# A two-layer trunk on one core: the second stage of a triangular inversion as a pipeline over four groups, and the values' convolution as a step of its own

## The chip, the cores and the metric

The kernel runs on one core of a Trainium2 chip. Its engines are PE (TensorE, matrix products), DVE (VectorE), ACT (ScalarE), POOL (GpSimd) and SP (SyncE, which starts DMA transfers). The metric is the device time of one execution in microseconds (us).

## The reference

Two layers act on 256 tokens of width 2048 in float32: h = h + Mixer(RMSNorm(h)). Layer 0 is a gated DeltaNet with 16 heads of 128, layer 1 is chunked softmax attention. What matters here is layer 0, cut to its core:

```python
proj = h @ w_in                                  # q, k, v, gate z, decay a, beta b
qkv  = silu(causal_depthwise_conv(qkv, conv_w))  # 4 taps
q, k = l2_norm(q) * 128 ** -0.5, l2_norm(k)
lower = where(tri_strict, (k * beta) @ k.T * decay, 0)
sol  = triangular_solve(eye + lower, rhs)        # rhs: v * beta and k * beta * exp(gc)
...
o = rms_norm(o, out_norm_w) * silu(z)
h = h + o @ w_out
```

The kernel solves over blocks of 128 tokens instead of 64: with two blocks for each of 16 heads it needs the inverses of 32 unit lower-triangular matrices of 128 x 128.

## The kernel before, in words

All weight products read 512 KB chunks of weights. `fetch` loads one (L208), ACT casts it to its high part (`whi`, L209) and DVE subtracts to get the low part (`wlo`, L210). Four load buffers and three of each part rotate, so a cast into a `whi` buffer waits until PE has used the chunk that was there three chunks earlier. The products themselves are all recorded at L259. In the stage of interest each chunk is of kind "half": 8 matmuls of 512 columns with `whi`, and 8 of 256 columns with `wlo`.

Everything else ("small work") is written as generators. `tick` and `step` take one piece of them after every part of a chunk, in turn from two lists, `bgq` and `bg2`; `drain()` takes pieces until both lists are empty. A list scheduler then sets each engine's final order; within an engine instructions run in that order.

`inversion()` has two stages. The first (L654 to L670) inverts the four 32 x 32 blocks on the diagonal of all 32 matrices on DVE. The second joins them:

- `lower` products (L684): 32 x 32 products of the matrix's off-diagonal blocks with the inverted blocks, two per matrix, on the array's tiles (0, 32) and (64, 96). DVE scales them into `v1` (L689).
- copies of the inverted blocks into the result `tt` and its transposed part `t64` (L696, L698), by ACT and POOL.
- corner products (L706, L708): three 32 x 32 products per matrix, from `v1`, on three tiles; ACT copies them to `tt` and `t64` (L713, L715). L706 writes one PSUM tile, L708 another.
- first quarter product (L723): a 64 x 64 product per matrix on tile (0, 64), from `t64`; DVE scales it into `v2` (L725).
- second quarter product (L731): 64 x 64 on tile (64, 0), from `v2` and `tt`; ACT copies the result to `tt` (L733).

Lower and corner products go in two groups of 16 matrices, each quarter pass in four groups of 8, one pass after the other. PE records every one of these float32 products as two matmuls, so 64 products stand as x128 in the profile.

After the inversion come the values. For each group of four heads, `pair` computes 512 columns of the projection, `v_small` convolves them (`conv`, L527 and L529), applies SiLU (L779), transposes (L786), scales by the key norms (L788), multiplies by the inverses `tt` (L795) and corrects the second block (L802, L805). `v_back` forms the output (L818 to L820), squares and normalises it (L821 to L830, L844 or L836), and `gated` transposes (L856) and splits it (L860, L861) for the output projection. For the last group the gate is multiplied in `za_small` (L752). After the first `pair` of values the main program calls `drain()`. The output projection's first products need heads 0 to 11 and are followed by those that need heads 12 to 15.

Of the kernel before, what the change touches and what calls it, by code (L numbers as in the profile page):

```python
# [10 lines left out]
AF = mybir.ActivationFunctionType  # L11
ALU = mybir.AluOpType
# [27 lines left out]
def tile_hybrid_trunk(  # L40
# [12 lines left out]
    act, dve, pool, pe = nc.scalar, nc.vector, nc.gpsimd, nc.tensor  # L53
# [9 lines left out]
    def ps_small():  # L63
        return pss.tile([P, 512], F32, name="pss", tag="pss")
# [19 lines left out]
    ps = ps_small()  # L84
# [169 lines left out]
    def drain():  # L254
        while now or bgq or bg2:
            step()
# [380 lines left out]
    def inversion():  # L637
        m = imem["m"]
        m1 = m[:, :4096].rearrange("p (k a b) -> p k a b", k=4, a=32)
        m2 = m[:, 4096:]  # L640
        tt = slot("tt", 16).rearrange("p (a c) -> p a c", c=P)
        tmem["tt"] = tt
        stg, lb, xb, tmp = (m1[:, i] for i in range(4))
        xr = m2[:, 0:1024].rearrange("p (a b) -> p a b", b=32)
        xt = m2[:, 1024:2048].rearrange("p (a b) -> p a b", b=32)
        t64 = m2[:, 2048:4096].rearrange("p (a b) -> p a b", b=64)
        yield from gather(12, H)
        xbf = xb.rearrange("p a b -> p (a b)")
# [24 lines left out]

        def diag(hh, r0, c0, n):
            c0 += T * (hh % 2)
            return dl[r0:r0 + n, hh // 2, 0, c0:c0 + n]


        for q0 in range(0, 32, 16):
            ps = ps_small()  # L680
            for i in range(16):
                for b in (0, 2):
                    r, c = 32 * b, 32 * b + 32
                    pe.matmul(ps[c:c + 32, i * 32:(i + 1) * 32], lhsT=diag(q0 + i, r, c, 32),  # L684
                              rhs=xr[r:r + 32, q0 + i, :], start=True, stop=True, tile_position=(r, c))
                if i == 7:
                    yield 1
            for c in (32, 96):
                dve.tensor_tensor(out=v1[c:c + 32, q0:q0 + 16, :],  # L689
                                  in0=ps[c:c + 32].rearrange("p (a b) -> p a b", b=32),  # L690
                                  in1=nbr_f[c:c + 32, q0:q0 + 16].unsqueeze(2).broadcast_to([32, 16, 32]),
                                  op=ALU.mult)
            yield 1
            for b in (2 * (q0 // 16), 2 * (q0 // 16) + 1):
                pr = slice(32 * b, 32 * b + 32)
                (pool.tensor_copy if b % 2 else act.copy)(out=tt[pr, :, 32 * b:32 * b + 32], in_=xt[pr])  # L696
                if b < 2:
                    act.copy(out=t64[pr, :, 32 * b:32 * b + 32], in_=xr[pr])  # L698
                yield 1
        for q0 in range(0, 32, 16):  # L700
            ps, ps2 = ps_small(), ps_small()
            for i in range(16):
                hh = q0 + i
                for b in (0, 2):
                    r, c = 32 * b, 32 * b + 32
                    pe.matmul(ps[r:r + 32, i * 32:(i + 1) * 32], lhsT=v1[c:c + 32, hh, :],  # L706
                              rhs=xt[c:c + 32, hh, :], start=True, stop=True, tile_position=(c, r))
                pe.matmul(ps2[32:64, i * 32:(i + 1) * 32], lhsT=xt[32:64, hh, :], rhs=v1[32:64, hh, :],  # L708
                          start=True, stop=True, tile_position=(32, 32))
                if i % 4 == 3 and i < 15:  # L710
                    yield 1
            for r in (0, 64):
                act.copy(out=tt[r:r + 32, q0:q0 + 16, r + 32:r + 64],  # L713
                         in_=ps[r:r + 32].rearrange("p (a b) -> p a b", b=32))
            act.copy(out=t64[32:64, q0:q0 + 16, 0:32], in_=ps2[32:64].rearrange("p (a b) -> p a b", b=32))  # L715
            yield 1
            yield 1

        v2 = m1[64:128].rearrange("p k a b -> p (k a b)")[:, 0:2048].rearrange("p (a b) -> p a b", b=64)
        for q0 in range(0, 32, 8):  # L720
            ps = ps_small()
            for i in range(8):
                pe.matmul(ps[64:128, i * 64:(i + 1) * 64], lhsT=diag(q0 + i, 0, 64, 64), rhs=t64[0:64, q0 + i, :],  # L723
                          start=True, stop=True, tile_position=(0, 64))
            dve.tensor_tensor(out=v2[:, q0:q0 + 8, :], in0=ps[64:128].rearrange("p (a b) -> p a b", b=64),  # L725
                              in1=nbr_f[64:128, q0:q0 + 8].unsqueeze(2).broadcast_to([64, 8, 64]), op=ALU.mult)
            yield 1
        for q0 in range(0, 32, 8):
            ps = ps_small()
            for i in range(8):  # L730
                pe.matmul(ps[0:64, i * 64:(i + 1) * 64], lhsT=v2[:, q0 + i, :], rhs=tt[64:128, q0 + i, 64:128],  # L731
                          start=True, stop=True, tile_position=(64, 0))
            act.copy(out=tt[0:64, q0:q0 + 8, 64:128], in_=ps[0:64].rearrange("p (a b) -> p a b", b=64))  # L733
            yield 1
        pool.tensor_scalar(out=epq, in0=ssq, scalar1=EPS, scalar2=EPS * P, op0=ALU.add, op1=ALU.mult)


# [30 lines left out]
                step()  # L768
        return pre

    def v_small(gi, ps):
        for cv in conv(ps, 32 + 4 * gi):
            yield 1
        if gi == 0:
            gated_tiles()
        vb, vs, on, sq = (dl_work(k) for k in range(4))
        tt, l01, z = tmem["tt"], dl[:, :, 0, P:2 * P], zmem["z"]
        h0 = 4 * gi
        act.activation(out=cv, in_=cv, func=AF.Silu)  # L779
        yield 1  # L780
        yield 1
        for p in range(2):
            ps = ps_small()
            for i in range(2):
                for t in range(2):
                    pe.transpose(ps[:, i * T + t * P:i * T + (t + 1) * P],  # L786
                                 cv[:, 2 * p + i, t * P:(t + 1) * P], ident)
            dve.tensor_tensor(out=vb[:, 2 * p:2 * p + 2], in0=ps.rearrange("p (h t d) -> p h t d", h=2, t=2),  # L788
                              in1=rk[:, h0 + 2 * p:h0 + 2 * p + 2, :].unsqueeze(3).broadcast_to([P, 2, 2, P]),
                              op=ALU.mult)  # L790
        yield 1
        for t in range(2):
            ps = ps_small()
            for i in range(4):
# [16 lines left out]
    def v_back(gi):  # L811
# [3 lines left out]
        for p in range(2):  # L815
            for i in (2 * p, 2 * p + 1):
                a, o = dec[:, h0 + i, :], po[p][:, (i % 2) * T:(i % 2 + 1) * T]
                pe.matmul(o[:, 0:P], lhsT=a[:, 0:P], rhs=vs[:, i, 0, :], start=True, stop=True)  # L818
                pe.matmul(o[:, P:T], lhsT=a[:, P:T], rhs=vs[:, i, 0, :], start=True, stop=False)
                pe.matmul(o[:, P:T], lhsT=a[:, T:T + P], rhs=vs[:, i, 1, :], start=False, stop=True)  # L820
            act.activation(out=sq[:, 2 * p:2 * p + 2], in_=po[p].rearrange("p (h t d) -> p h t d", h=2, t=2),  # L821
                           func=AF.Square)
        yield 1

        so = tiny.tile([P, 4, 2], F32, name="so", tag="so")
# [58 lines left out]
        bg2.append(za_small(gi, block("tokens", xb, 2)))  # L884
    for gi in range(4):
        ps = pair(xb, 2)
        if gi == 0:
            drain()
        bgq.append(v_small(gi, ps))
    bgq.append(za_small(3, block("tokens", xb, 2)))  # L890


# [318 lines left out]
```

## Time and profile before

| | |
|---|---|
| median of 3 timed runs | 1014.46 us (1013.89 to 1014.59) |
| profiled execution, first to last instruction (its span) | 1012.6 us |
| PE, matmuls | 1003.2 us, x6090 |
| PE, weight loads | 881.2 us, x6090 |
| DVE | 688.4 us, x1117 |
| ACT | 525.8 us, x778 |
| mean granted PE clock | 0.997 |

The profile gives the profiled execution's span but no other time for it; the three timed runs are executions of their own. PE's matmuls overlap: a matmul's row shows the time from its start to its modelled end, so the distance from start to start tells what it costs. The inversion's second stage lies between about 298 and 332 us of the span, the values' steps between 332 and 470.

### The profile page before, as it was taken

To read this page: it belongs to the slowest core of one execution; us is meant where nothing else is said; L and a number is where in the kernel's file an instruction comes from. 1 tells how busy PE (TensorE), PEld (TensorE's weight loads), DVE (VectorE), ACT (ScalarE), POOL (GpSimd) and SP (SyncE) were. 2 spreads that over 40 slices of the span, in tenths; PEclk is the share of its full clock that TensorE was granted. 3 is DMA by queue.
4 is the path that set the end of the run, shared out by engine and by line. 5 is a ranking of instruction groups with operands and counts; after the bars stand their busy time and mean duration, and the time that the engine had idled before them with its cause. 6 is when DMAs were issued, how large, how long until landed. Compare 5 with 4: busy or idle time off the path is not lost.

```text
span 1012.6 us, 15650 instructions
## 1 busy us (share of the span) xinstructions
PE 1003.2 (99%) x6090; PEld 881.2 (87%) x6090; DVE 688.4 (68%) x1117; ACT 525.8 (52%) x778; POOL 64.7 (6%) x83
## 2 busy tenths in 40 slices
PE   8999999999998999999999999999999999999998
PEld 7988888888887989899988888888888888889987
DVE  7789879997997587755866555444456665666554
ACT  7467865564454455444654444444445555555432
POOL 1000001131000011001000000000011010101000
PEclk9999999999998999999999999999999999999999
DMA  9665665555754454546756776666665555555472
GB/s 307 166 170 157 173 180 154 152 160 155 205 165 122 125 162 132 164 146 194 234 179 184 225 214 207 193 200 189 193 187 177 150 170 163 166 152 161 156 232 91
DMA packets 134186, 177.57 MB, mean 175 GB/s; under 512 B 7904, under 2 KB 90208, under 8 KB 134112
## 3 DMA queue, kind: packets, MB, share of 16 engines
q1 hardware_dynamic: 132672, 172.12, 57.4%
q0 software_dynamic: 1152, 4.19, 1.2%
q8 instruction: 47, 0.77, 0.3%
q10 hardware_dynamic: 288, 0.26, 0.1%
q14 instruction: 27, 0.22, 0.1%
HBM read 174.46 MB, written 2.10 MB: 174 GB/s over the span
## 4 chain that ended last, share of the span: by engine, by line
PE 97%; DVE 1%; issue 1%; DMA 1%; SPq 0%; ACT 0%; DVEq 0%
PE psp L259 85%; PE pss L601 2%; PE pss L259 1%; PE pss L795 1%; PE pss L1030 1%; PE pss L1049 1%; PE pss L1085 1%; DMA wt<-in_a_w_in_dram 1%; PE pss L501 1%; PE pss L1075 1%; PE pss L723 0%; PE pss L731 0%; DVE wlo L210 0%; PE pss L786 0%; PE pss L818 0%
## 5 line engine op out<-in xcount | busy, mean ns | idle before, releaser
L210 DVE TENSOR_TENSOR wlo<-wt,whi 128x1024 fp32r<-128x1024 f32 (+1 forms) x322 | 390.9, 1217 | 243.3 <-ACT whi L209 240.5
L209 ACT CAST whi<-wt 128x1024 fp32r<-128x1024 f32 (+1 forms) x322 | 336.5, 1046 | 386.3 <-PE psp L259 326.9
L259 PE MATMUL psp<-whi,xb 128*128 128x512 f32 x1024 | 318.7, 391 | 0.0
L259 PE MATMUL psp<-xb,whi 128*128 128x512 f32 (+1 forms) x1088 | 260.9, 382 | 1.3 <-ACT whi L209 0.7
L259 PEld LDWEIGHTS psp<-xb,whi 128*128 128x128 f32 x1088 | 196.1, 190 | 35.8 <-ACT whi L209 1.2
L259 PEld LDWEIGHTS psp<-whi,xb 128*128 128x128 f32 x1024 | 191.8, 188 | 39.1
L259 PE MATMUL psp<-wlo,xb 128*128 128x512 f32 x512 | 200.9, 392 | 0.0
L259 PE MATMUL psp<-xb,wlo 128*128 128x256 f32 x1024 | 148.9, 285 | 0.8 <-DVE wlo L210 0.8
L259 PE MATMUL psp<-g,whi 128*128 128x256 f32 (+1 forms) x736 | 149.5, 318 | 0.0
L259 PEld LDWEIGHTS psp<-xb,wlo 128*128 128x128 f32 x1024 | 138.4, 193 | 6.3 <-DVE wlo L210 1.0
L259 PEld LDWEIGHTS psp<-g,whi 128*128 128x128 f32 x736 | 121.5, 191 | 8.2
L259 PEld LDWEIGHTS psp<-wlo,xb 128*128 128x128 f32 x512 | 96.1, 188 | 19.7
L259 PE MATMUL psp<-g,wlo 128*128 128x256 f32 x480 | 101.9, 284 | 0.0
L259 PEld LDWEIGHTS psp<-g,wlo 128*128 128x128 f32 x480 | 77.8, 191 | 1.1
L529 DVE SCALAR_TENSOR_TENSOR cv<-raw,sm,cv 128x255 f32<-128x255 f32 (+2 forms) x144 | 62.8, 475 | 5.8 <-ACT cv L527 5.7
L527 ACT ACTIVATE cv<-raw,sm 128x256 f32<-128x256 f32 x48 | 22.1, 508 | 20.0 <-DVE raw L345 19.9
L1013 POOL TENSOR_SCALAR ssn<-ssn,uh 128x4 f32<-128x4 f32 x16 | 8.3, 529 | 266.8 <-DVE ssn L1011 266.8
L330 DVE TENSOR_TENSOR ev<-psp,ev 128x512 f32<-128x512 f32 x33 | 22.5, 681 | 0.0
L329 ACT COPY ev<-psp 128x512 f32<-128x512 f32 x33 | 19.1, 578 | 0.0
L830 POOL TENSOR_TENSOR ro<-so,nhalf 128x8 f32<-128x8 f32 x4 | 9.0, 2248 | 151.9 <-DVE so L828 151.9
L1061 ACT ACTIVATE raw<-raw,mx 128x128 f32<-128x128 f32 (+1 forms) x32 | 14.2, 445 | 7.4 <-DVE mx L1059 7.4
L605 DVE TENSOR_TENSOR dl<-pss,dl 128x512 f32<-128x512 f32 (+1 forms) x32 | 16.3, 549 | 2.7 <-PE pss L601 2.7
(233 smaller groups left out, 743.3 us busy)
## 6 DMA issues: line engine op xcount, KB each, us to landing
wt<-in_b_w_in_dram SPq DMA_DIRECT2D x128, 512.0 KB, 3.8
wt<-in_a_w_in_dram SPq DMA_DIRECT2D x127, 512.0 KB, 4.0
wt<-in_a_w_out_dram SPq DMA_DIRECT2D x32, 512.0 KB, 3.8
wt<-in_b_w_out_dram SPq DMA_DIRECT2D x32, 512.0 KB, 3.8
dl<-in_xT_dram POOLq DMA_DIRECT2D x4, 512.0 KB, 6.1
dl<-in_relb_dram POOLq DMA_DIRECT2D x4, 512.0 KB, 5.2
g<-in_xT_dram SPq DMA_DIRECT2D x7, 256.0 KB, 5.5
out_dram<-cv SPq DMA_DIRECT2D x2, 512.0 KB, 3.2
```

What stands on the lines that cost most here:

```text
L209: cast = act.copy(out=hi[:, js, cs], in_=wt[:, js, cs])
L210: rest = dve.tensor_tensor(out=lo[:, js, cs], in0=wt[:, js, cs], in1=hi[:, js, cs].bitcast(F32), op=ALU.subtract)
L259: state["mm"] = pe.matmul(*args, **kw).ins
L329: act.copy(out=ev, in_=ps[:, :, 1, :])
L330: dve.tensor_tensor(out=ev, in0=ps[:, :, 0, :], in1=ev, op=ALU.add)
L501: pe.matmul(dst, lhsT=lhs, rhs=rbuf[:, gi % 2, 2 * half + part, :], start=(part == 0), stop=(part == 1))
L527: act.activation(out=cv[:, i, :], in_=raw[:, i, :], func=AF.Copy, scale=conv_w(i0 + i, 3))
L529: dve.scalar_tensor_tensor(out=cv[:, i, s:], in0=raw[:, i, :T - s], scalar=conv_w(i0 + i, 3 - s), in1=cv[:, i, s:], op0=ALU.mult, op1=ALU.add)
L601: pe.matmul(dst, lhsT=kq[:, a, i, c:c + P], rhs=rhs, start=(n == 0), stop=(n == 2))
L605: dve.tensor_tensor(out=dl[:, h, :, c], in0=src.rearrange("p (k c) -> p k c", k=2), in1=dec[:, h, c].unsqueeze(1).broadcast_to([P, 2, n]), ...
L795: pe.matmul(ps[:, i * P:(i + 1) * P], lhsT=tt[:, 2 * (h0 + i) + t, :], rhs=vb[:, i, t, :], start=True, stop=True)
L1061: act.activation(out=s[:, a:b], in_=s[:, a:b], func=AF.Exp, bias=mx[:, t:t + 1], accum_out=sums[:, t:t + 1])
```

## The change

The second stage becomes four groups of 8 matrices. In round n it runs the quarter products for group n - 2 (first pass) and group n - 3 (second pass), then the corners of group n - 1, then the lower products of group n. The two quarter passes of a round alternate matrix by matrix and write the two halves of one PSUM tile. The third corner product now shares a PSUM tile with the other two. The copies of the diagonal blocks come in the first round. The convolution and SiLU of the values are a generator of their own, `v_conv`, in list `bg2`; `v_rest` holds the other steps and waits for it. `vmem` keeps the two within two groups of one another. The call of `drain()` after the first `pair` is gone.

```diff
-        for q0 in range(0, 32, 16):
-            ps = ps_small()
-            for i in range(16):
-                for b in (0, 2):
-                    ...
...
+        def lower(g):
+            q0 = 8 * g
+            ps = ps_small()
+            for i in range(8):
+                for b in (0, 2):
+                    r, c = 32 * b, 32 * b + 32
+                    pe.matmul(ps[c:c + 32, i * 32:(i + 1) * 32], lhsT=diag(q0 + i, r, c, 32),
+                              rhs=xr[r:r + 32, q0 + i, :], start=True, stop=True, tile_position=(r, c))
...
+        def corners(g):
...
-                pe.matmul(ps2[32:64, i * 32:(i + 1) * 32], lhsT=xt[32:64, hh, :], rhs=v1[32:64, hh, :],
+                pe.matmul(ps[32:64, i * 32:(i + 1) * 32], lhsT=xt[32:64, hh, :], rhs=v1[32:64, hh, :],
...
+        def quarters(g3, g4):
+            ps = ps_small()
+            for i in range(8):
+                cs = slice(i * 64, (i + 1) * 64)
+                if g3 is not None:
+                    hh = 8 * g3 + i
+                    pe.matmul(ps[64:128, cs], lhsT=diag(hh, 0, 64, 64), rhs=t64[0:64, hh, :],
+                              start=True, stop=True, tile_position=(0, 64))
+                if g4 is not None:
+                    hh = 8 * g4 + i
+                    pe.matmul(ps[0:64, cs], lhsT=v2[:, hh, :], rhs=tt[64:128, hh, 64:128],
+                              start=True, stop=True, tile_position=(64, 0))
+                if i == 3:
+                    yield 1
...
+        for n in range(7):
+            if n >= 2:
+                yield from quarters(n - 2 if n < 6 else None, n - 3 if n > 2 else None)
+            if 1 <= n <= 4:
+                yield from corners(n - 1)
+            if n < 4:
+                yield from lower(n)
+            if n == 0:
+                yield from copies()
...
-    def v_small(gi, ps):
+    vmem = {"turned": -1, "back": -1}
+    def v_conv(gi, ps):
+        while vmem["turned"] < gi - 2:
+            yield 1
         for cv in conv(ps, 32 + 4 * gi):
             yield 1
+        act.activation(out=cv, in_=cv, func=AF.Silu)
+        vmem[gi] = cv
+        yield 1
+    def v_rest(gi):
+        while gi not in vmem:
+            yield 1
...
     for gi in range(4):
         ps = pair(xb, 2)
-        if gi == 0:
-            drain()
-        bgq.append(v_small(gi, ps))
+        bg2.append(v_conv(gi, ps))
+        bgq.append(v_rest(gi))
```

In the changed kernel the lower products are L697 (scaled at L702), the corners L716 and L718 (copied at L723 and L725), the first quarter pass L735 (scaled at L745), the second L739 (copied at L748), the values' transposes L821, the product with the inverses L833, and the gate's transposes L895. L209, L210, L259, L329, L330, L345, L527 and L529 keep their numbers. An order row counts one product where the profile has two matmuls.

PE before, from the first lower products into the corners (rows with `whi` are matmuls of a weight chunk's high part, with `wlo` of its low part):

```order
L259 MATMUL psp<-xb,whi 128x512 x16
L684 MATMUL pss<-g,dl 32x32 x64
L259 MATMUL psp<-xb,wlo 128x256 x16
L259 MATMUL psp<-xb,whi 128x512 x11
L706 MATMUL pss<-g 32x32
L708 MATMUL pss<-g 32x32 x3
L706 MATMUL pss<-g 32x32 x7
```

PE of the changed kernel at the same place:

```order
L697 MATMUL pss<-g,dl 32x32 x16
L259 MATMUL psp<-xb,wlo 128x256 x16
L259 MATMUL psp<-xb,whi 128x512 x8
L716 MATMUL pss<-g 32x32
L697 MATMUL pss<-g,dl 32x32
L716 MATMUL pss<-g 32x32
L718 MATMUL pss<-g 32x32
L716 MATMUL pss<-g 32x32 x2
```

Before, all 64 lower products stand in one run and all 96 corner products in another, with 27 of L259 between them; now a run of 16 lower products comes first and, 24 of L259 later, a run of 24 corners and 16 lower products.

PE before, at the quarter products:

```order
L259 MATMUL psp<-xb,wlo 128x256 x12
L723 MATMUL pss<-g,dl 64x64 x32
L259 MATMUL psp<-xb,wlo 128x256 x4
L259 MATMUL psp<-xb,whi 128x512 x13
L731 MATMUL pss<-tt,g 64x64 x32
L786 MATMUL pss<-ident,cv 128x128 x4
```

PE of the changed kernel, in the third and fourth of the runs of small products (the fourth has the first alternating quarters; the corners are L716 and L718):

```order
L697 MATMUL pss<-g,dl 32x32 x16
L259 MATMUL psp<-xb,whi 128x512 x12
L259 MATMUL psp<-xb,wlo 128x256 x9
L735 MATMUL pss<-g,dl 64x64
L259 MATMUL psp<-xb,wlo 128x256 x3
L739 MATMUL pss<-tt,g 64x64
L735 MATMUL pss<-g,dl 64x64
L739 MATMUL pss<-tt,g 64x64
```

The two passes were runs of 32 products each; now 8 products of the first pass stand alone, then three runs hold 8 of each pass in turn (followed by 24 corners and 16 lower products in the first, 24 corners in the second), and 8 of the second pass stand alone at the end.

DVE before, from the first lower products on (`v1` and `v2` are in `g`):

```order
L210 TENSOR_TENSOR wlo<-wt,whi 128x1024 x2
L689 TENSOR_TENSOR g<-pss,nbr 32x512 x4
L210 TENSOR_TENSOR wlo<-wt,whi 128x1024
L345 TENSOR_TENSOR raw<-ev,rB 128x512
L210 TENSOR_TENSOR wlo<-wt,whi 128x1024
L330 TENSOR_TENSOR ev<-psp,ev 128x512
```

DVE of the changed kernel there:

```order
L210 TENSOR_TENSOR wlo<-wt,whi 128x1024
L702 TENSOR_TENSOR g<-pss,nbr 32x256 x2
L210 TENSOR_TENSOR wlo<-wt,whi 128x1024 x2
L345 TENSOR_TENSOR raw<-ev,rB 128x512
L210 TENSOR_TENSOR wlo<-wt,whi 128x1024
L702 TENSOR_TENSOR g<-pss,nbr 32x256 x2
L330 TENSOR_TENSOR ev<-psp,ev 128x512
```

The scaling of the lower products was one run of four pieces behind two splits; now the first two pieces stand behind one split, and the next two behind three more splits and a piece of the values' scaling.

More of the change, by code (lines that the diff above doesn't have):

```diff
@@ L676, in diag, with copies @@
             return dl[r0:r0 + n, hh // 2, 0, c0:c0 + n]
-        for q0 in range(0, 32, 16):
-            ps = ps_small()
-            for i in range(16):
-                for b in (0, 2):
[L683 to L694, printed above, removed]
+        v2 = m1[64:128, 2:4].rearrange("p k a b -> p (k a b)").rearrange("p (a b) -> p a b", b=64)
+        def copies():
+            for b in range(4):
                 pr = slice(32 * b, 32 * b + 32)
@@ L699, in inversion @@
                 yield 1
-        for q0 in range(0, 32, 16):
-            ps, ps2 = ps_small(), ps_small()
-            for i in range(16):
+        def lower(g):
[8 more added lines that the diff above has]
+                    yield 1
+            for c in (32, 96):
+                dve.tensor_tensor(out=v1[c:c + 32, q0:q0 + 8, :],
+                                  in0=ps[c:c + 32, :256].rearrange("p (a b) -> p a b", b=32),
+                                  in1=nbr_f[c:c + 32, q0:q0 + 8].unsqueeze(2).broadcast_to([32, 8, 32]),
+                                  op=ALU.mult)
+            yield 1
+        def corners(g):
+            q0 = 8 * g
+            ps = ps_small()
+            for i in range(8):
                 hh = q0 + i
@@ L707, in inversion @@
                               rhs=xt[c:c + 32, hh, :], start=True, stop=True, tile_position=(c, r))
-                pe.matmul(ps2[32:64, i * 32:(i + 1) * 32], lhsT=xt[32:64, hh, :], rhs=v1[32:64, hh, :],
+                pe.matmul(ps[32:64, i * 32:(i + 1) * 32], lhsT=xt[32:64, hh, :], rhs=v1[32:64, hh, :],
                           start=True, stop=True, tile_position=(32, 32))
-                if i % 4 == 3 and i < 15:
+                if i in (2, 5):
                     yield 1
             for r in (0, 64):
-                act.copy(out=tt[r:r + 32, q0:q0 + 16, r + 32:r + 64],
-                         in_=ps[r:r + 32].rearrange("p (a b) -> p a b", b=32))
@@ L715, in inversion @@
-            act.copy(out=t64[32:64, q0:q0 + 16, 0:32], in_=ps2[32:64].rearrange("p (a b) -> p a b", b=32))
+                act.copy(out=tt[r:r + 32, q0:q0 + 8, r + 32:r + 64],
+                         in_=ps[r:r + 32, :256].rearrange("p (a b) -> p a b", b=32))
+            act.copy(out=t64[32:64, q0:q0 + 8, 0:32], in_=ps[32:64, :256].rearrange("p (a b) -> p a b", b=32))
             yield 1
-            yield 1
-        v2 = m1[64:128].rearrange("p k a b -> p (k a b)")[:, 0:2048].rearrange("p (a b) -> p a b", b=64)
@@ L720, in inversion @@
-        for q0 in range(0, 32, 8):
+        def quarters(g3, g4):
             ps = ps_small()
             for i in range(8):
[L723 to L726, printed above, removed]
-            yield 1
@@ L728, in inversion @@
[L728 to L734, printed above, removed]
+                cs = slice(i * 64, (i + 1) * 64)
[3 more added lines that the diff above has]
+                              start=True, stop=True, tile_position=(0, 64))
@@ new lines, in quarters @@
+                if g4 is not None:
+                    hh = 8 * g4 + i
+                    pe.matmul(ps[0:64, cs], lhsT=v2[:, hh, :], rhs=tt[64:128, hh, 64:128],
+                              start=True, stop=True, tile_position=(64, 0))
+                if i == 3:
+                    yield 1
+            if g3 is not None:
+                hs = slice(8 * g3, 8 * g3 + 8)
+                dve.tensor_tensor(out=v2[:, hs, :], in0=ps[64:128].rearrange("p (a b) -> p a b", b=64),
+                                  in1=nbr_f[64:128, hs].unsqueeze(2).broadcast_to([64, 8, 64]), op=ALU.mult)
@@ new lines, in quarters @@
+            if g4 is not None:
+                act.copy(out=tt[0:64, 8 * g4:8 * g4 + 8, 64:128],
+                         in_=ps[0:64].rearrange("p (a b) -> p a b", b=64))
+            yield 1
+        for n in range(7):
[7 more added lines that the diff above has]
+                yield from copies()
@@ L769, in ready @@
         return pre
-    def v_small(gi, ps):
+    vmem = {"turned": -1, "back": -1}
+    def v_conv(gi, ps):
+        while vmem["turned"] < gi - 2:
+            yield 1
         for cv in conv(ps, 32 + 4 * gi):
             yield 1
+        act.activation(out=cv, in_=cv, func=AF.Silu)
+        vmem[gi] = cv
+        yield 1
+    def v_rest(gi):
+        while gi not in vmem:
+            yield 1
+        cv = vmem[gi]
         if gi == 0:
@@ L778, in v_small @@
         h0 = 4 * gi
-        act.activation(out=cv, in_=cv, func=AF.Silu)
-        yield 1
-        yield 1
         for p in range(2):
@@ L790, in v_small @@
                               op=ALU.mult)
+        vmem["turned"] = gi
         yield 1
+        while vmem["back"] < gi - 1:
+            yield 1
         for t in range(2):
@@ L822, in v_back @@
                            func=AF.Square)
+        vmem["back"] = gi
         yield 1
```

## The prediction

> **What bounds the kernel now.** I read the page first, then the waits of PE (TensorE), the chain around the inversion's second stage, and its PE timeline. The page's busy shares, and one DMA queue of its section 3 (packets, MB, share):
>
> ```profile
> PE 1003.2 (99%) x6090; PEld 881.2 (87%) x6090; DVE 688.4 (68%) x1117; ACT 525.8 (52%) x778; POOL 64.7 (6%) x83
> q8 instruction: 47, 0.77, 0.3%
> ```
>
> PE is busy 99% of the span, so it is the bound. A change to this kernel pays only where PE waits, runs at a lower clock, or spends its own time badly. The longest wait of PE over the run (total us, times, longest):
>
> ```profile
> PE pss L706 <- issue: 2.9, 1, 2.9
> ```
>
> It falls on L706, in the lines that the change rewrites. The chain from 300 to 336 us (start, us, what), then windows there (us, busy by engine, granted clock, DMA share, GB/s):
>
> ```profile
> 303.16 2.14 PE pss L684 x128
> 305.30 4.62 PE psp L259 x27
> ...
> 311.90 2.86 issue
> 314.76 0.26 PE pss L706 x2
> ...
> 315.41 4.99 PE psp L259 x17
> 320.40 4.01 PE pss L723 x64
> ...
> 328.06 3.87 PE pss L731 x64
> ```
>
> ```profile
> 303.10:311.90 8.80, 8.80 (x324) 7.92 (x323) 7.53 (x10) 4.34 (x7) 0.00 (x0) 1.00 0.74 213
> 311.90:314.80 2.90, 0.04 (x4) 0.04 (x5) 2.90 (x8) 1.33 (x3) 0.00 (x0) 0.84 0.86 236
> 314.80:320.70 5.90, 5.90 (x44) 5.13 (x45) 1.75 (x5) 3.57 (x6) 0.00 (x0) 0.50 0.03 9
> ```
>
> PE stands for 2.86 us with no releaser shown, and then has half the clock until 320.7 (0.50 in the third window). The second cost is as large as the first and the busy share hides it.
>
> What was it waiting for? Queue q8 moved 47 packets of 0.77 MB: 16 KB each, one per 259 of the 12180 matmuls and weight loads of PE. So q8 is PE's own instruction stream, in blocks of some 256. From 303.1 to 311.9 PE took 324 + 323 = 647 instructions, 2.5 blocks, and of them, behind the 128 matmuls of L684 and the 27 of L259, 169 matmuls with their loads, 338, in the last 2 us. What q8 moved from 305.9 to 312.0, and from 311.9 to 314.8:
>
> ```profile
> q8 instruction: 1, 0.02, 0.9%
> ```
>
> ```profile
> q8 instruction: 1, 0.02, 2.0%
> ```
>
> One block came in the first window; the next came inside the stall. I read the stall as PE having run through its instructions faster than they arrive. A block of 128 matmuls went by in about 1.5 us there (169 in 2.0) and the stall added 2.9, so I estimate that PE needs about 4.4 us per block not to starve.
>
> **The change part by part.** The timeline of PE (start, us, what) prices the rest:
>
> ```profile
> 293.77 3.82 PE L259 MATMUL psp<-xb,whi 128*128 128x512 f32 x16
> 297.43 2.08 PE L259 MATMUL psp<-xb,wlo 128*128 128x256 f32 x16
> 299.34 3.81 PE L259 MATMUL psp<-xb,whi 128*128 128x512 f32 x16
> 303.09 2.21 PE L684 MATMUL pss<-g,dl 32*32 32x32 f32 x128
> 305.23 2.17 PE L259 MATMUL psp<-xb,wlo 128*128 128x256 f32 x16
> 307.24 2.68 PE L259 MATMUL psp<-xb,whi 128*128 128x512 f32 x11
> ...
> 311.60 0.19 PE L708 MATMUL pss<-g 32*32 32x32 f32 x1
> 311.62 0.20 PE L706 MATMUL pss<-g 32*32 32x32 f32 x2
> 311.63 0.19 PE L708 MATMUL pss<-g 32*32 32x32 f32 x1
> ```
>
> From start to start, 16 of 512 columns take 3.66 us (0.229 each) and 16 of 256 take 1.91 (0.119 each).
>
> *The stall goes: +2.9 us.* In the new order no run of small products exceeds 112 matmuls (16 + 24 + 16 products, each two matmuls in the trace), that is 224 instructions, and between runs stand 23 to 31 of L259. The tightest 128 matmuls I can lay over the order are one such run (about 2.35 us) and the 16 L259 before it (3 + 9 of 256 columns, 4 of 512: 2.35 us): 4.7 us, just above 4.4. Bounds: 0 to 2.9 saved; I take 2.9, since even the worst block fits.
>
> *The half clock goes with it: +2.9 us.* The 17 L259 after the stall are 5 of 512 and 12 of 256 columns: 5 x 0.229 + 12 x 0.119 = 2.57 us at full clock against 4.99 measured, 2.42 lost. The last 24 small matmuls took 0.65 (314.76 to 315.41) for some 0.3, and L723 took 4.01 where L731 of the same shape took 3.87: together 0.5 more. No idle, no lower clock; bounds 0 to 2.9.
>
> *The 64-column passes in pairs: +2.8 us.* L731 gives 3.87 us for 64 matmuls, one after the other on one quadrant; less 0.15 for edges, 58 ns each. In the new order 96 of the 128 stand as 48 pairs on opposite quadrants (the first and the last group of eight have no partner). No row shows 64-wide pairs. The nearest are the 32-wide ones: L708 recurs every 32 ns while two L706 on other tiles run in the same 32 ns, so three tiles cost what one does. If pairs behave so, 48 x 58 ns = 2.8 us goes. Bounds 0 and 2.8; I take 2.8.
>
> Against that part stands a rule of the Trainium skill (TensorEngine Tiling, Gotcha 1): different row tiles cannot access the same PSUM bank at once, and the new quarters write both passes into one bank. By that rule the pairs would save nothing and the sum would be 3.9. The rows speak against it: the two L706 at 311.62 are different row tiles of one bank, and both start within 0.01 us though each is 0.19 long (ends are modelled, so this is no proof for 64 columns).
>
> *More changes of tile shape: -1.7 us.* Going into L684 cost 0.09 (299.34 to 303.09 is 3.75, for 3.66); after it L259's 16 of 256 columns took 2.01 for 1.91; its own 2.14 holds 0.1 over 64 x 32 ns. So about 0.3 per excursion from 128-wide work. There were four; the new order has eight, and three more switches between 64 and 32 within them. 4 x 0.3 = 1.2, and three between 0 and 0.3, at 0.15: 0.5. Bounds 1.2 to 2.1.
>
> *Eviction pieces: nothing on the path.* Eight DVE pieces of 256 columns replace four of 512, twelve ACT copies replace six (groups by line and shape: busy us, mean ns, idle before):
>
> ```profile
> L689 DVE TENSOR_TENSOR g<-pss,nbr 32x512 f32<-32x512 f32 x4 | 2.8, 690 | 0.1
> L605 DVE TENSOR_TENSOR dl<-pss,dl 128x256 f32<-128x256 f32 x16 | 6.6, 414 | 0.0
> L209 ACT CAST whi<-wt 128x1024 fp32r<-128x1024 f32 x319 | 335.1, 1051 | 385.6 <-PE psp L259 326.9 <-issue 32.7 <-DVE cv L1020 4.9
> L210 DVE TENSOR_TENSOR wlo<-wt,whi 128x1024 fp32r<-128x1024 f32 x319 | 389.4, 1223 | 242.6 <-ACT whi L209 239.7 <-PE psp L259 2.3
> ```
>
> DVE: 8 x 0.414 - 2.8 = 0.5 us more; ACT some 1.4 more at 0.41 a copy. What hides it is L259 between hand-offs. I walked the queues with the durations above. The hand-off to the second corners is typical. Its DVE piece L702 stands behind the split L210 of a weight chunk, that behind ACT's cast L209, that behind PE's last use of the buffer, just before the first corners. PE gets there at 303.1 + 0.8 (first lower group) + 3.8 (24 of L259) = 307.7, and the matmul's own 0.4 ends at 308.1; with 1.05 for the cast, 1.22 for the split and 0.83 for two L702 that is 311.2. PE asks for it after the first corners with the next lower group (1.4) and 28 of L259 (4.6): 313.7. Every hand-off so walked leaves 2 us or more. If that cover is gone, PE waits; that is the slow rival.
>
> *No drain, convolution apart: nothing but the tail.* The convolution's scalar pieces move between the new small ones on DVE and ACT; PE's list of L259 stays whole. The value steps begin some 16 us of L259 later than before, and the last heads' gate ends later. Of before, its tail in the chain and on DVE, PE and ACT:
>
> ```profile
> 457.49 10.07 PE psp L259 x84
> ...
> 463.94 1.28 DVE L752 TENSOR_TENSOR dl<-dl,kT 128x512 f32<-128x512 f32 x2
> ...
> 467.40 0.38 PE L856 MATMUL pss<-ident,dl 128*128 128x128 f32 x2
> ...
> 468.10 0.82 PE L856 MATMUL pss<-ident,dl 128*128 128x128 f32 x6
> 468.62 1.27 ACT L860 ACTIVATE g<-pss,sm 128x512 fp32r<-128x512 f32 x2
> ```
>
> L752 ended 2.18 us before the transposes; the new order has 76 L259 there for 84, so 1.0 less, which still fits. But behind the last six transposes now come only 9 L259 (1.1 us) before PE needs the gated heads. From the first of the six to the end of the first DVE piece behind L860 I reckon 0.52 (468.10 to 468.62) + 0.64 (half of 1.27) + 0.69 (512 columns, as L689) = 1.9 us, against PE's 0.6 + 1.1 + 0.12 = 1.8. So -0.2, bounds 0 to -0.6.
>
> Sum: 2.9 + 2.9 + 2.8 - 1.7 - 0.2 = 6.7 us. The profiled execution's span is 1012.6, 1.9 under the median of the timed runs, 1014.46; I take that difference as unchanged. 1014.46 - 6.7 = 1007.8 us.
>
> **The rivals.** *The stall was not the instruction stream.* Then it stays, wherever the small products stand, and the half clock with it: 2.8 - 1.7 - 0.2 = 0.9 saved, 1013.5 us. For it: the profile names no releaser, and "issue" names nothing. Against it: the block that arrives inside the stall, and 338 instructions in the 2 us before. A rule of the Trainium skill points this way (Runtime: NRT & Kernel Launch, Instruction fetch mechanics): fetch is hidden, because the sequencer dispatches more slowly than blocks are filled. By that rule the stall would not be fetch; the trace has 2.86 us that look like it. Chance 0.10.
>
> *The pairs do not overlap*: 6.7 - 2.8 = 3.9 saved, 1010.6 us. Chance 0.10.
>
> *Switches cost nothing more, or corners and lower products overlap as well*: 6.7 + 1.7 = 8.4 and a little more, 1005.5 to 1006 us. Chance 0.09.
>
> *Slower: hand-offs in DVE's and ACT's queues.* Each of four groups now crosses PE to DVE to PE to ACT to PE to DVE to PE, behind weight casts and convolution pieces. If one hand-off comes late by as much as the stall did, the clock falls again: 2.9 + 2.9. One such stall leaves 0.9 of the gain; two turn it to 6.7 - 11.6 = -4.9: 1019.4 us. It decides from about 5 us later than I walked it (2 of cover and a stall of 2.9), twice. For it: L210 behind L209 behind PE is the longest dependence here. Against it: 2 us of cover at each. Chance 0.05.
>
> **How the numbers follow.** The forecast has 0.66, with 1006.3 to 1009.5 as its own range. The range 1005.5 to 1011.5 takes in the pairs' rival and the cheap switches and leaves out the persisting stall and the slow case, 0.15, and some edge. About 0.2% (2 us) is what a measurement of this kernel can tell from no change; the persisting stall falls within it. Faster 0.66 + 0.10 + 0.09 = 0.85; within 0.10; slower 0.05.
>
> **What would show it.** Right: no wait of PE on "issue" near 312, granted clock 1.00 in every window from 303 to 345, and a group of 32 paired 64-column matmuls in about 1 us. Wrong: a wait of PE on DVE L702 or L745 or ACT L723 of over 2 us; a second stretch at 0.50; pairs that take 2 us per group (the bank rule); or the "issue" wait again with a block of q8 inside it.

## Result, and the profile after

| | before | after |
|---|---|---|
| median of 4 runs, us | 1014.52 | 1008.8 |
| lowest and highest, us | 1013.89, 1014.59 | 1008.57, 1010.83 |
| span of the profiled execution, us | 1012.6 | 1009.1 (its time: 1010.83) |
| first lower product to end of span, us | 1012.6 - 303.16 = 709.4 | 1009.1 - 305.70 = 703.4 |

The ratio is 0.9946, 95% interval 0.9934 to 0.9958: 5.7 us faster, where 6.7 were forecast. The last row of the table leaves out the start, which varies by a microsecond or two between executions; from there to the end the gain is 6.0 us. In the rest of this document that stretch is the measure. Each value is that of one profiled execution; in the two pairs of kernels that run the same instructions there without a stall it came out the same within 0.1 us (703.9 and 703.9, 703.4 and 703.4 in the table of the experiments).

What the start does to the profiled execution of after, from its timeline (with the wait in brackets) and its windows (us, busy PE, granted clock, DMA share, GB/s):

```profile
11.22 0.80 PE L259 MATMUL psp<-xb,whi 128*128 128x256 f32 x2 [1.95 <-ACT whi L209]
```

```profile
10.70:17.60 6.90, 5.91 (x26) 0.51 1.03 347
17.60:30.00 12.40, 12.40 (x105) 1.00 0.90 268
```

PE waited 1.95 us for a weight cast and had half the clock from 10.74, inside that wait, to 17.57. The change does not touch that part; before its run had waits of 0.70 and 0.76 there and no half clock. That fits this execution's 2 us above the other three, whose mean clocks are 1.000, 1.000 and 0.998 against its 0.997; no trace of theirs was kept.

PE's waits of after from 296 us to the end (total us, times, longest), and windows over the changed stage:

```profile
PE psp L259 <- DVE wlo L210: 0.3, 1, 0.3
PE psp L259 <- DVE ev L330: 0.2, 1, 0.2
```

```profile
303.00:330.00 27.00, 27.00 (x434) 1.00 0.56 157
330.00:345.00 15.00, 15.00 (x194) 1.00 0.49 142
```

The wait on "issue" is gone, and so is the window at 0.50. The chain of after through the stage (start, us, what):

```profile
305.70 0.62 PE pss L697 x32
306.32 3.94 PE psp L259 x24
...
311.31 4.88 PE psp L259 x28
316.19 1.07 PE pss L735 x16
...
318.32 4.02 PE psp L259 x21
322.34 0.26 PE pss L735 x2
322.59 0.55 PE psp L259 x3
```

Between the groups of small products stand 4 to 5 us of L259: this is what the pipeline does to the instruction stream. By the traces, the fastest 128 matmuls in a row (256 instructions with their weight loads) take 1.35 us from start to start where the order is that of before (in before with 154 more, which has no stall), and 4.67 us in after, from 321.10 on. And the two 64-column passes, L735 and L739, in PE's timeline:

```profile
323.18 0.22 PE L739 MATMUL pss<-tt,g 64*64 64x64 f32 x1
323.19 0.22 PE L735 MATMUL pss<-g,dl 64*64 64x64 f32 x1
323.24 0.22 PE L739 MATMUL pss<-tt,g 64*64 64x64 f32 x1
323.24 0.22 PE L735 MATMUL pss<-g,dl 64*64 64x64 f32 x1
```

A matmul of each pass starts every 58 ns or so, in the same hundredth of a microsecond as its partner, into one accumulator tile. One wait inside the values was not forecast (timeline of after):

```profile
442.73 0.69 DVE L823 TENSOR_TENSOR dl<-pss,rk 128x512 f32<-128x512 f32 x1 [1.26 <-PE pss L821]
443.33 1.22 DVE L210 TENSOR_TENSOR wlo<-wt,whi 128x1024 fp32r<-128x1024 f32 x1
...
444.60 0.38 PE L259 MATMUL psp<-g,wlo 128*128 128x256 f32 x1 [0.35 <-DVE wlo L210]
```

DVE took the key scale L823 first, which itself waited for PE's transposes; the split of a weight chunk stood behind it, and PE came 0.35 us early. From the start of the matmul ahead of it (the last of L833, 443.98) to its own start are 0.62 us, where such a product takes 0.11: the wait costs 0.5 us.

### The profile page after: what moved, and what is told of

Read it like the earlier page. It is cut to its first block, busy times and chain, and to the rows that moved or that the text cites. A ratio compares the mean times of both kernels' runs of the same rounds, so it can differ in the third digit from the quotient of the medians.

```text
span 1009.1 us, 15660 instructions
## 1 busy us (share of the span) xinstructions
PE 1001.4 (99%) x6090; PEld 878.8 (87%) x6090; DVE 690.0 (68%) x1121; ACT 526.6 (52%) x784; POOL 62.4 (6%) x83
## 4 chain that ended last, share of the span: by engine, by line
PE 98%; DMA 1%; DVE 0%; ACT 0%; issue 0%; SPq 0%
PE psp L259 87%; PE pss L601 2%; PE pss L259 1%; PE pss L1068 1%; DMA wt<-in_a_w_in_dram 1%; PE pss L1087 1%; PE pss L1123 1%; PE pss L833 1%; PE pss L501 1%; PE pss L1113 1%; PE pss L857 0%; PE pss L856 0%; PE pss L840 0%; PE pss L858 0%; PE pss L1086 0%; PE pss L1124 0%
## 5 line engine op out<-in xcount | busy, mean ns | idle before, releaser
L210 DVE TENSOR_TENSOR wlo<-wt,whi 128x1024 fp32r<-128x1024 f32 (+1 forms) x322 | 391.2, 1218 | 244.9 <-ACT whi L209 241.0
L209 ACT CAST whi<-wt 128x1024 fp32r<-128x1024 f32 (+1 forms) x322 | 336.7, 1046 | 381.3 <-PE psp L259 331.8
L259 PE MATMUL psp<-whi,xb 128*128 128x512 f32 x1024 | 318.9, 391 | 0.0
L259 PE MATMUL psp<-xb,whi 128*128 128x512 f32 (+1 forms) x1088 | 261.4, 382 | 2.2 <-ACT whi L209 1.9
L259 PEld LDWEIGHTS psp<-xb,whi 128*128 128x128 f32 x1088 | 197.0, 191 | 36.4 <-ACT whi L209 2.5
L259 PEld LDWEIGHTS psp<-whi,xb 128*128 128x128 f32 x1024 | 191.7, 188 | 39.1
L259 PE MATMUL psp<-wlo,xb 128*128 128x512 f32 x512 | 200.8, 392 | 0.0
L259 PE MATMUL psp<-xb,wlo 128*128 128x256 f32 x1024 | 149.0, 285 | 0.7 <-DVE wlo L210 0.7
L259 PE MATMUL psp<-g,whi 128*128 128x256 f32 (+1 forms) x736 | 149.6, 318 | 0.0
L259 PEld LDWEIGHTS psp<-xb,wlo 128*128 128x128 f32 x1024 | 138.0, 192 | 6.6 <-DVE wlo L210 1.2
L259 PEld LDWEIGHTS psp<-g,whi 128*128 128x128 f32 x736 | 121.7, 191 | 8.4 <-DVE g L900 0.2
L259 PEld LDWEIGHTS psp<-wlo,xb 128*128 128x128 f32 x512 | 96.2, 188 | 19.7
L259 PE MATMUL psp<-g,wlo 128*128 128x256 f32 x480 | 101.9, 284 | 0.3 <-DVE wlo L210 0.3
L259 PEld LDWEIGHTS psp<-g,wlo 128*128 128x128 f32 x480 | 77.8, 191 | 1.7 <-DVE wlo L210 0.5
L529 DVE SCALAR_TENSOR_TENSOR cv<-raw,sm,cv 128x255 f32<-128x255 f32 (+2 forms) x144 | 63.8, 477 | 3.4 <-ACT cv L527 3.2
L527 ACT ACTIVATE cv<-raw,sm 128x256 f32<-128x256 f32 x48 | 22.5, 509 | 20.6 <-DVE raw L345 20.6
L330 DVE TENSOR_TENSOR ev<-psp,ev 128x512 f32<-128x512 f32 x33 | 22.6, 684 | 0.1
L329 ACT COPY ev<-psp 128x512 f32<-128x512 f32 x33 | 19.1, 579 | 0.0
L1058 DVE TENSOR_TENSOR cv<-psp,rn 128x512 f32<-128x512 f32 x16 | 10.2, 683 | 8.9 <-POOL rn L1053 8.9
```

The lines of the kernel that those rows point to most:

```text
L209: cast = act.copy(out=hi[:, js, cs], in_=wt[:, js, cs])
L210: rest = dve.tensor_tensor(out=lo[:, js, cs], in0=wt[:, js, cs], in1=hi[:, js, cs].bitcast(F32), op=ALU.subtract)
L259: state["mm"] = pe.matmul(*args, **kw).ins
L329: act.copy(out=ev, in_=ps[:, :, 1, :])
L330: dve.tensor_tensor(out=ev, in0=ps[:, :, 0, :], in1=ev, op=ALU.add)
L527: act.activation(out=cv[:, i, :], in_=raw[:, i, :], func=AF.Copy, scale=conv_w(i0 + i, 3))
```

## The experiments

Two theories stood against each other. The one of the prediction: PE's instructions come in blocks of 256, a block passed in under about 4.4 us leaves PE without instructions, and half the clock follows. Its rival: the stall belongs to the place, that is to the tensors and queues at the corners. The first five experiments add instructions on PE ahead of everything, as a warm-up of more and narrower matmuls, and leave the order of all else as it is on every engine. That shifts the borders of the blocks, and nothing else in the stage. The theory forecasts a different stall for each shift.

Where the stage starts and ends in each profiled execution, with the span's end (us):

```
kernel                                first small product   span    between
before                                303.16                1012.6  709.4
before, 256 instructions more         303.91                1014.0  710.1
before, 154 more                      303.95                1007.8  703.9
before, 128 more                      304.72                1008.6  703.9
before, 190 more                      303.62                1008.8  705.2
before, 202 more                      303.31                1008.9  705.6
after                                 305.70                1009.1  703.4
after, 154 more                       304.20                1007.6  703.4
after, passes one after the other     303.45                1008.7  705.2
after, values as before               304.71                1008.6  703.9
before, 154 more, pairs               303.69                1007.4  703.7
before, 154 more, values as after     303.56                1007.8  704.2
```

### 256 instructions more: the control

```diff
-    for _ in range(NWARM):
-        pe.matmul(ps, lhsT=warm[:, :P], rhs=warm, start=True, stop=True)
+    for _ in range(140):
+        pe.matmul(ps[:, :32], lhsT=warm[:, :P], rhs=warm[:, :32], start=True, stop=True)
```

> The kernel before with 140 narrow warm-up matmuls in place of its 12 wide ones: 128 pairs of weight load and matmul, 256 instructions, more on TensorE ahead of everything, nothing else moved. Theory (instructions are fetched in blocks of 256, and a block that runs out in less than about 4.4 us stalls TensorE for the rest): 256 more instructions leave the borders where they were, so the stall of 2.86 us stands at the same place, after the 168th of the 192 small products L706/L708, and the half clock behind it too; the stage from the lower products L684 to the end of L731 takes what it took, within 0.3 us. Rival (the stall belongs to something else at that place, the tensors or the queues): the same. The run is the control for the other three; the total moves only by what the start does, within 2 us.

Measured: 1015.37 us, 1.0009 of before (1.0000 to 1.0019). Chain, then window behind the stall:

```profile
312.66 3.32 issue
```

```profile
316.00:322.00 6.00, 6.00 (x45) 0.50 0.02 4
```

The stall stands at the same matmul, and half the clock behind it. It is 0.5 us longer than in before, so 4.4 us is not a fixed figure. The stage, from the first lower product to the end of L731, takes 0.6 us more than in before (303.91 to 333.29 against 303.16 to 331.94), where 0.3 at most was expected. The other warm-up by itself takes nothing away.

### 154 more: no block that runs out

The same edit with 89 matmuls of 48 columns.

> The kernel before with 89 narrow warm-up matmuls in place of its 12 wide ones: 154 more TensorE instructions ahead of everything, nothing else moved. Theory (blocks of 256): the borders move 154 instructions towards the start, so that each block holds a stretch of large products of over 4 us: no stall, an issue wait of at most 0.2 us in the stage, and so no half clock (1.00 between 303 and 345 us); the time falls by 5.8 us to about 1008.7, give or take the start. If the half clock was not the stall's doing, it stays and the time is 1011.6. Rival (the stall belongs to the place, not to the instruction stream): 2.86 us at the same matmul, 1014.5.

Measured: 1009.92 us, 0.9953 of before (0.9938 to 0.9968). Windows over the place of the stall:

```profile
303.00:312.00 9.00, 9.00 (x281) 1.00 0.68 187
312.00:316.00 4.00, 4.00 (x111) 1.00 0.83 242
316.00:330.00 14.00, 14.00 (x165) 1.00 0.28 78
```

No wait, no half clock, and 709.4 - 703.9 = 5.5 us gone, with before's own inversion and values; 5.8 were expected. The rival is refuted: tensors, queues and order at the place are as they were. The half clock was the stall's doing: without the wait it did not come.

### 190 more: a short stall elsewhere

The same edit with 107 matmuls of 40 columns.

> The kernel before with 107 narrow warm-up matmuls in place of its 12 wide ones: 190 more TensorE instructions. Theory: a block border falls about nine large products behind the last of L706/L708 and the border ahead of it 3.2 us earlier, so the stall is 4.4 - 3.2 = 1.2 us (0.8 to 1.6) and stands among the large products L259 there; none among L706/L708. Half clock: probably none after so short a wait, which gives 1009.9; with it 1012.8. Rival (the place, not the stream): 2.86 us after the 168th of L706/L708, 1014.5.

Measured: 1010.53 us, 0.9958 of before (0.9944 to 0.9973). Chain, then window:

```profile
312.62 1.83 PE psp L259 x9
314.45 1.08 issue
315.52 1.22 PE psp L259 x8
```

```profile
315.60:322.00 6.40, 6.40 (x80) 1.00 0.02 4
```

The stall has moved out of the small products into the large ones behind nine of them, where the border was put, with 1.08 us for a forecast of 1.2. Behind this wait the clock stayed at 1.00.

### 128 more: a miss

The same edit with 76 matmuls of 64 columns.

> The kernel before with 76 narrow warm-up matmuls in place of its 12 wide ones: 128 more TensorE instructions, half a block. Theory: one block now begins with the first of the 64 lower products L684 and runs out with the last of them 2.06 us later, so the stall moves there: none among L706/L708, and 4.4 - 2.06 = 2.3 us (2.0 to 2.6) between the end of L684 and the large products behind it. Whether 2.3 us of waiting still calls the half clock is open: with it the time is about 1014, without it 1011. Rival (the place, not the stream): 2.86 us after the 168th of L706/L708, nothing behind L684.

Measured: 1009.46 us, 0.9949 of before (0.9935 to 0.9964), and no stall anywhere. The chain, and what q8 moved from 300.0 to 304.5 us:

```profile
304.72 2.14 PE pss L684 x128
306.86 4.62 PE psp L259 x27
...
313.72 2.79 PE psp L259 x17
```

```profile
q8 instruction: 1, 0.02, 1.4%
```

I had counted the border at the first lower product, 304.72, and took it that a block is asked for once the array passes a border. This block moved before 304.5, ahead of the first lower product; in the trace its packet starts at 303.02. So PE's sequencer had passed the border before the array did. My reading is that the sequencer is ahead of the array by some instructions while the array works on large products, so that such a border costs less than the count on the array says. That is argued from this one packet; it was not tried by itself.

### 202 more: how long a wait calls the half clock

The same edit with 113 matmuls of 38 columns.

> The kernel before with 113 narrow warm-up matmuls: 202 more TensorE instructions, so that the border that cost 1.1 us of waiting with 190 more stands 12 instructions nearer to the corners, behind six large products instead of nine or twelve. Theory (the next block is there 4.4 us after the border before it was passed): the wait is about 1 us longer, 2.0 (1.7 to 2.4), among the large products behind the last of L706/L708. Whether it calls the half clock is open: a wait of 1.1 did not, one of 2.9 and one of 3.3 did. With it about 1013.5, without it 1011.2. Rival (the place, not the stream): 2.86 us after the 168th of L706/L708.

Measured: 1014.61 us over 10 runs, 1010.62 to 1018.39, 1.0009 of before (0.9996 to 1.0023). The profiled execution is the fastest of them:

```profile
313.20 1.49 issue
```

```profile
314.70:322.00 7.30, 7.30 (x86) 1.00 0.05 16
```

The wait is longer than with 190 more, as the theory has it, though 1.49 us is below the 1.7 to 2.4 forecast. With 1.49 us the clock stayed. The other nine runs have mean clocks of 0.991 to 1.000, and eight of them lie above 1012: most of them probably had a half clock somewhere, but no trace of theirs was kept. A half clock at the start, as in the profiled execution of after, would look the same in these numbers, so whether this wait can call it stays open.

The four traces with the wait show when it ends. The packet of the missing block starts on q8 at 312.26 us in before, and at 313.47, 312.91 and 312.42 with 256, 190 and 202 more; PE goes on at 314.76, 315.98, 315.52 and 314.69, which is 2.50, 2.51, 2.61 and 2.27 us later. So the wait ends a nearly fixed time after its block was sent for. Counted the same way, the block of 128 more, with its packet at 303.02, was there at some 305.5, before the lower products ended at 306.86.

### The two passes one after the other

```diff
             for i in range(8):
                 cs = slice(i * 64, (i + 1) * 64)
                 if g3 is not None:
...
+            for i in range(8):
+                cs = slice(i * 64, (i + 1) * 64)
                 if g4 is not None:
```

> The changed kernel with the two 64-column passes of a step written one after the other instead of in turn; the same products, groups and places. Theory (a pair of the two passes takes the time of one): 24 of the 32 heads lose their partner, the step takes 2.8 us more, and the time is 1011.6. Rival (two products of different row tiles into one accumulator tile do not overlap): no change, 1008.8. Nothing else should move: no issue wait, clock 1.00.

Measured: 1010.75 us, 0.9957 of before (0.9940 to 0.9974); from the first small product to the end 1.8 us more than after. A step in the chain, first and last row of its products, then PE's timeline where one pass meets the other (L735, then L741 in the program):

```profile
320.08 0.90 PE pss L735 x13
...
321.15 0.75 PE pss L741 x13
```

```profile
320.41 0.57 PE L735 MATMUL pss<-g,dl 64*64 64x64 f32 x7
320.76 0.27 PE L741 MATMUL pss<-tt,g 64*64 64x64 f32 x1
320.82 0.22 PE L735 MATMUL pss<-g,dl 64*64 64x64 f32 x1
320.87 0.22 PE L741 MATMUL pss<-tt,g 64*64 64x64 f32 x1
320.88 0.22 PE L735 MATMUL pss<-g,dl 64*64 64x64 f32 x1
320.93 0.22 PE L741 MATMUL pss<-tt,g 64*64 64x64 f32 x1
320.93 0.22 PE L735 MATMUL pss<-g,dl 64*64 64x64 f32 x1
320.99 0.68 PE L741 MATMUL pss<-tt,g 64*64 64x64 f32 x9
```

The pairs overlap: taken apart they cost more. But 2.8 was too much for this kernel, since PE overlaps the seam by itself: three of L741 start ahead of L735's last or with it, though in PE's order, as the list scheduler leaves it, all eight of L735 stand ahead of L741. A step took 1.82 us here (320.08 to 321.90) against 1.07 for eight pairs: 3 x 0.75 = 2.25 us. And this order has no lone pair at 322.34 with three L259 behind it, which costs after 0.26 + 0.55 - 3 x 0.119 = 0.45 us. 2.25 - 0.45 = 1.8.

### After with the values of before

The inversion of after, with the values' step, the drain and their queue as in before (the second half of the diff taken back).

> The changed kernel's inversion with the values of the kernel before (drain ahead of them, convolution inside the step). Theory (the values' part of the change gave nothing and cost a wait of 0.6 us for a split behind the key scale and one of 0.3 us at the end): both waits are gone, 1007.9, between 1007.4 and 1008.5. Rival (the drain held something back): the time is above the changed kernel's, 1009.4 or more, with a new wait of TensorE in the values.

Measured: 1009.40 us, 0.9943 of before (0.9928 to 0.9958), and 703.9 against 703.4. My theory fell: the time is not 1007.9. The rival fits the time (1009.4) and has a wait inside the values, though with the drain in place before with 154 more has no such wait. The chain of this kernel:

```profile
440.49 1.05 ACT whi L209
```

The cast takes 1.05 us, of which PE is idle for 0.3. So a wait inside the values is here too, at the gate's transposes and for a weight cast, where after waits for a split behind the key scale. It does not take the values' new order to bring one. What brings it was not tried.

### After with 154 more

After with the 89 warm-up matmuls.

> The changed kernel with the same 89 narrow warm-up matmuls that took the stall from the kernel before: 154 more TensorE instructions ahead of everything. Theory (all but a little of the change's gain is the stall and its half clock, which the other warm-up alone removes; the changed stage holds no block that runs out in 4.4 us wherever the borders lie): no stall here either, and what is left between the two is 2.8 (pairs) - 1.5 (more changes of tile shape) - 0.9 (the waits of the values) = 0.4 us: 1009.5 against 1009.9, where the changed kernel with its own warm-up has 1008.8. Rival (the pipeline gains by itself, whatever the borders): 5.7 us under the other warm-up too, 1004.2.

Measured: 1009.22 us, 0.9940 of before (0.9926 to 0.9955), against 1009.92 for before with the same warm-up. From the first small product to the end they have 703.4 and 703.9: a difference of 0.5 us, where 0.4 was forecast and the rival had 5.7. No "issue" wait: after is free of the stall with both places of the borders.

### Before with 154 more, and the pairs alone

```diff
-        for q0 in range(0, 32, 8):
-            ps = ps_small()
-            for i in range(8):
-                pe.matmul(ps[64:128, i * 64:(i + 1) * 64], lhsT=diag(q0 + i, 0, 64, 64), rhs=t64[0:64, q0 + i, :],
...
+        for n in range(5):
+            g3, g4 = (n if n < 4 else None), (n - 1 if n > 0 else None)
+            ps = ps_small()
+            for i in range(8):
```

> The kernel before with the 89 narrow warm-up matmuls (no stall) and of the change only the pairs: the lower products and the corners as they were, in blocks of 64 and 96, then the two 64-column passes in turn, one group apart, in six visits in place of two. Theory: pairs give 2.8 us, four more visits to the small tiles cost 0.3 us each, 1.2: 1008.3, where the same kernel without pairs has 1009.9. Rival (a visit costs nothing): 1007.1. Rival (pairs do not overlap): 1011.1.

Measured: 1009.55 us, 0.9947 of before (0.9932 to 0.9961); 703.7 against 703.9 without pairs, a gain of 0.2 us where 1.6 was forecast. Neither the theory nor a rival has that. Its chain at a visit with eight pairs:

```profile
322.14 0.20 PE pss L731
...
323.10 0.11 PE pss L731 x2
323.21 4.94 PE psp L259 x26
```

Eight pairs take 323.21 - 322.14 = 1.07 us, what eight lone products take (1.07 at 316.19 in after). The pairs do what they should, but only 0.2 us of it reaches the end. Counted from each matmul's start to the next, from the first small product to the end, and against before with 154 more: the 64-column products take 1.9 us less, L259 0.5 more and the 128-column products of the values 1.3 more. So the values lose most of it. The gate's transposes are the largest part, 3.7 us for 2.5: in the chain four of them (L862) take 0.78 us at 439.86, where one takes 0.11 in before with 154 more (L856, 432.89). Why they come later and wait is not settled.

### Before with 154 more, and the values' part alone

The second half of the diff, on before with the 89 warm-up matmuls.

> The kernel before with the 89 narrow warm-up matmuls (no stall) and of the change only the values' part: no drain, the convolution a step of its own; the inversion as before. From the start of the lower products to the end, 703.9 us without this part; the pipeline without the values' part has 704.0 and the whole change 703.5. Theory (the values' part gives its 0.5 us by itself): 703.5, and a time of 1009.5. Rival (it gives something only behind the pipeline): 703.9 or more, 1009.9. In either case no issue wait and the clock at 1.00.

Measured: 1010.25 us, 0.9959 of before (0.9945 to 0.9974); 704.2, so 0.3 us slower than without it, where behind the pipeline the same lines gave 0.5. Neither theory has that. What is left of the change besides the stall moves by up to half a microsecond in either direction from one of these kernels to the next. The order of L259 around the values differs in each of them; that this is the reason is not shown.

## Why the prediction was right, step by step

- *What q8 is, and the stall goes (+2.9).* Right, and shown: the wait moves with the number of instructions ahead (2.86, 3.32, 1.08, 1.49 or none), and not with the place. The Trainium skill's rule that fetch is hidden (Runtime: NRT & Kernel Launch, Instruction fetch mechanics) does not hold in this stage. That spreading the small products cures it is shown by the traces' count: a block takes at least 4.67 us in after, by the prediction's own count 4.7, and 1.35 in the order of before. That after has no wait with two places of the borders would not show it by itself, since before has none with two of its places either.
- *The half clock goes with it (+2.9).* Right. Both together were 5.5 us by the shift alone, where 5.8 were forecast; with 2.9 for the wait, 2.6 are left for the clock. The prediction reckoned 2.57 us at full clock for the 17 L259 behind the stall; at 154 more they take 2.79 there (312.95 to 315.74), so 2.2 of their 4.99 was lost, not 2.42.
- *Pairs (+2.8).* Right in mechanism and size: at full clock (before with 154 more) each of the two passes takes 3.87 us as 64 matmuls in a row, 0.97 for eight products, and three groups of eight now ride along at no cost, 2.9. The rule of the Trainium skill against it (TensorEngine Tiling, Gotcha 1, on row tiles in one bank) does not show in the rows at 323.18.
- *Tile shapes (-1.7).* Of the right size, by an estimate from two rows. In the 64-column visits it is 0.8: five visits of 1.07 and the lone pair of 0.26 (L735 at 322.34, one of the eight visits of the forecast) make 5.6, 2.1 less than 7.74 and not 2.9. The 32-column products take as long as they did, 4.4 us in all. The rest falls on L259: the 24 of it at 306.32 take 3.94 for 16 x 0.119 + 8 x 0.229 = 3.74, so 0.2 a visit and 0.8 for four more. Together 1.6.
- *Hand-offs and eviction pieces (0).* No wait of PE on L702, L723 or L745. The slow rival did not come.
- *The values (-0.2 at the tail).* Too small. Two L259 that wait for the last gated heads take 0.71 us at 473.12, where two like them take 0.40 just ahead:

```profile
472.76 0.40 PE L259 MATMUL psp<-g,whi 128*128 128x256 f32 x2
...
473.12 0.71 PE L259 MATMUL psp<-g,whi 128*128 128x256 f32 x2
```

  That is 0.3. The wait at 444.60, 0.5 us, was in no term: I had walked the hand-offs of the inversion, not those of the values.

Forecast without stall and clock: 2.8 - 1.7 - 0.2 = 0.9; measured 703.9 - 703.4 = 0.5. With the pairs at 2.9 and the shapes at 1.6, the values cost about 0.8 where 0.2 stood: the wait at 444.60 and the tail of 0.3 make that up. So the term that was mis-sized most is the values'. Nine tenths of the gain is the stall with its half clock. The rest of the rewrite is worth half a microsecond here, and a warm-up with other numbers gives before nearly the whole gain. What the rewrite has ahead of it is that no shift of the code should bring more than a trace of the stall back: the densest block of after takes 4.67 us, where the blocks that came late came some 3.9 to 4.8 us after the border (estimated below). Only two shifts of after were run.

## What to carry to other kernels

A wait of TensorE on nothing, in a run of a few hundred tiny matmuls, is worth testing with a pad of instructions ahead of it: if the wait moves or goes, it is the instruction stream. Then spread the tiny matmuls among large ones, and count how long the fastest 128 matmuls in a row still take. Price the clock behind a wait along with the wait. Where a change removes such a stall, measure the same alignment without the change before crediting the rest of it.

## What the runs showed of the hardware

- The length of a wait does not by itself say whether the half clock (0.50) comes. In the stage, waits of 1.08 and 1.49 us left the clock at 1.00, and 2.86 and 3.32 us brought 0.50. At the program's start 1.95 us brought it in after, and 1.54 and 0.76 in after with the values of before, but 1.78 and 0.76 left 1.00 in after with 154 more. Two waits of 0.76 brought it in before with 128 more; 0.70 and 0.76 in before did not. What else decides is open. Each time it lasted 6.83 us or half of that, and in before it began 1.9 us into the wait. Windows of before (the stage) and of after, before with 128 more and after with the values of before (the start), then the wait without a half clock:

```profile
313.84:320.67 6.83, 5.91 (x44) 0.50 0.17 58
10.74:17.57 6.83, 5.88 (x26) 0.50 1.03 345
11.74:15.15 3.41, 3.41 (x17) 0.50 1.04 384
13.28:16.69 3.41, 3.41 (x19) 0.50 1.03 316
```

```profile
11.24 0.50 PE L259 MATMUL psp<-xb,whi 128*128 128x256 f32 x2 [1.78 <-ACT whi L209]
9.00:30.00 21.00, 18.01 (x146) 1.00 0.98 311
```

- A block of 256 instructions was there some 4.3 to 4.8 us after the border ahead of it had been passed. I estimate it as the wait and the time of the 256 instructions before it: 2.86 + 1.5 in before, 3.32 + 1.5 in the control, 1.08 + 1.83 + 1.4 at 190 more (119 corner matmuls at the pace of 169 in 2.0 us). At 202 more it comes out lower, 1.49 + 0.90 + 1.5 = 3.9; it is not one figure. What is nearly one is the time from the packet's start to PE going on, 2.27 to 2.61 us in the four.
- TensorE starts products of another tile up to three places ahead of its order (320.76 in the kernel with the passes one after the other), so two passes written one after the other overlap at the seam by 0.18 us: 8 x 0.117 = 0.93 for a second pass by itself, 1.82 - 1.07 = 0.75 measured.
